# Depthwise convolution taps without diagonal products: ScalarE's products summed by accumulating transfers

## The chip, the core and the metric

The kernel runs on one core of one Trainium2 chip. Its engines are TensorE (PE; matmuls into PSUM), VectorE (DVE), ScalarE (ACT), GpSimd (POOL) and SyncE (SP, which issues transfers); each takes its instructions in the order of its own queue and waits where an operand is not there. The metric is the device time of one execution in microseconds, lower is better.

## What is computed

A trunk of two layers over a sequence of 1024 frames with 1024 channels, all in float32. Layer 0 mixes with a Conformer convolution module, layer 1 with chunkwise retention; each is followed by a squared-ReLU MLP of width 4096, and each sub-layer is normed and modulated by a conditioning vector. What the change touches is in layer 0:

```
u = h @ w_pw1 + b_pw1                     # 1024 -> 2048
a, g = split(u);  u = a * sigmoid(g)      # gate
u = depthwise causal convolution of u over 31 frames, per channel, + b_dw
u = silu(layernorm(u) * ln_g + ln_b)
y = u @ w_pw2 + b_pw2
x = x + g1 * y;  h = modulate(rmsnorm(x));  x = x + g2 * (relu(h @ w1)**2 @ w2)
```

## The kernel before

Channels lie on the 128 partitions, in 8 tiles; frames lie along a row, in two halves of 512. A float32 matmul is made of three: every weight block of 128 x 1024 is loaded by SP into `raw` (2 buffers), cast by ACT to a high part (L522), subtracted to a low part (L523), both into `whl` (9 buffers, two for a block), and `mm3` issues high x high, high x low and low x high (L258 to L260).

The first projection (pw1) makes, for a channel tile j and a half t, one unit `("u", j, t)`: 24 matmuls for the value, 24 for the gate, a sigmoid (L690) and the product (L699) that writes the unit's row, with 30 frames of the past ahead of it. The 31 taps of a unit are products of a shifted row with one weight per channel. Before, four engines share them:

- TensorE: the first `NPE[t][j]` taps as a matmul with a diagonal matrix, which ACT writes from the identity (`dg`, L718, L721), into a PSUM tile `acc`.
- VectorE: the middle taps, multiplied and added in one instruction (L730 begins a chain, L733 goes on), in two chains with a PSUM tile each.
- ACT and POOL: the last `NPOOL[t][j]` taps; ACT multiplies (`cacc` for the first, `prod` for the others, L738) and POOL adds each `prod` to `cacc` (L741).
- VectorE joins: `cacc` plus the first chain (L743), then plus the second, into the unit's own row (L744).

The 8 units of half 0 then go through the layer norm (mean, L753; scaling, L758), the second projection (pw2; its product is added to x in L782) and the MLP, of which 7 of 8 blocks run for half 0 alone (`mlp`: L804 to L809 make the hidden tiles, L818 adds to x) while the taps of half 1 are made. Modulation vectors are dot products of a 128 x 1024 block of `ada` with the condition: on VectorE in one instruction (L555), or on POOL (L552) with the sum on ACT (L553).

The order of all this is not written out: `Plan` takes every operation with an engine, a planned duration, a priority from the table `PR` and the buffers it needs (`RINGS`), plays them against each other, and issues them in the order that comes out. `NPOOL` and `NPE` share out the taps; `WPOOL` says that every n-th weight subtraction of a kind goes to POOL (0: none; `w1` there are the six pw1 blocks that are loaded a second time for half 1, so every 8th of them is none either); `M0POOL`, `M1POOL` and `MODPOOL` do the same for the dot products.

Of the kernel before, what the change touches and what calls it, by code (L numbers as in the profile page):

```python
# [58 lines left out]
PR = dict(h0=dict(A=504, V=930), x1=dict(D=1069, step=4), n1=dict(P=576, A=282, V=324), w0=dict(A=612, V=412, D=687, step=32), pw1=dict(P=778, step=0), glu=dict(A=841, V=327, G=591, step=32), taps0=dict(A=786, V=468, G=153, step=4), pw1h1=dict(P=1185, step=2), w1=dict(A=304, V=255, G=86, D=205, step=32), glu1=dict(A=252, V=67, step=0), halo=dict(A=354, step=2), dg=dict(P=989, step=16), mod2=dict(A=274, V=38, G=538, D=444, step=32), ln0=dict(P=555, A=52, V=38, step=2), y0=dict(D=218), pw2=dict(P=636, A=636, V=345, step=1), pw2w=dict(A=84, V=172, G=902, D=390, step=2), mod3=dict(A=488, V=349, G=92, D=558), nm0=dict(P=548, A=629, V=480, step=1), mod5=dict(A=322, V=96, G=271, D=571, step=4), mlp=dict(P=1064, A=793, V=339, G=552, D=587, step=0), taps1=dict(A=688, V=517, G=953), ln1=dict(P=690, A=1116, V=450, step=0), y1=dict(D=441), pw21=dict(P=615, A=508, V=193, step=2), pw2w1=dict(A=746, V=962, G=879, D=616, step=1), nm1=dict(P=328, A=268, V=867, step=0), m0=dict(A=641, V=571, G=43, D=769, step=1), m1=dict(A=486, V=187, G=818, D=0, step=1), wf=dict(A=976, V=291, D=847, step=32), G=dict(V=869, step=4))  # L59
WPOOL = dict(w0=0, w1=8, pw2=0, mlp=0, pw21=0)  # L60
M0POOL = (1, 2, 3)
M1POOL = (0, 4, 7)
# [4 lines left out]
class Plan:
# [139 lines left out]
class Trunk:  # L207
# [263 lines left out]
    def layer_conv(self):  # L471
# [236 lines left out]
        def taps(j, t, p):

            npool, npe = NPOOL[t][j], NPE[t][j]  # L710
            u = ("u", j, t)
# [4 lines left out]
            for s in range(npe):
                dg = k("dg", s)
                inorder("dg", "A", 0.293, p, lambda s=s, dg=dg: nc.scalar.activation(E[dg], self.ident, AF.Identity, scale=wv(s)),  # L718
                        r=["const"], w=[dg], a={dg: ("dg", dict(cols=P))})
# [1 line left out]
                inorder("acc" if s == 0 else ("pe", t, j), "P", 0.907, ("dg", 0), lambda s=s, dg=dg: nc.tensor.matmul(  # L721
                    E[k("acc", 0)], E[dg], sl(s), start=s == 0, stop=s == npe - 1), r=[dg, u], w=[k("acc", 0)], **first)
            begun = [npe > 0, False]
            for i, s in enumerate(range(npe, nd)):
                c = i % 2
                a = k("acc", c)
                if not begun[c]:
                    begun[c] = True
                    bias = self.v("b_dw", j) if c else 0.0
                    inorder("acc", "V", 0.68, p, lambda s=s, a=a, bias=bias: nc.vector.tensor_scalar(E[a], sl(s), wv(s), bias, ALU.mult, ALU.add),  # L730
                            r=[u, "const"], w=[a], a={a: ("acc", {})})
                else:
                    op("V", 0.68, p, lambda s=s, a=a: nc.vector.scalar_tensor_tensor(E[a], sl(s), wv(s), E[a], ALU.mult, ALU.add), r=[u], w=[a])  # L733
            ca = k("cacc")
            for i, s in enumerate(range(nd, TAPS)):
                pr = ca if i == 0 else k("prod", s)
                kind = "cacc" if i == 0 else "prod"
                inorder(kind, "A", 0.613, p, lambda s=s, pr=pr: nc.scalar.activation(E[pr], sl(s), AF.Identity, scale=wv(s)),  # L738
                        r=[u, "const"], w=[pr], a={pr: (kind, {})})
                if i:  # L740
                    op("G", 1.28, p, lambda pr=pr: nc.gpsimd.tensor_tensor(E[ca], E[ca], E[pr], ALU.add), r=[pr], w=[ca])  # L741
# [1 line left out]
            op("V", 0.62, p, lambda: nc.vector.tensor_tensor(E[ca], E[ca], E[a0], ALU.add), r=[a0], w=[ca])  # L743
            op("V", 0.62, p, lambda: nc.vector.tensor_tensor(E[u][:, :HALF], E[ca], E[a1], ALU.add), r=[ca, a1], w=[u])  # L744
# [569 lines left out]
```

## Time and profile before

| what | value |
|---|---|
| median of 3 runs | 2701.77 us (2699.62 to 2702.38) |
| the profiled execution | 2705.48 us, span 2703.6 us, mean granted TensorE clock 0.985 |
| busy of the span, PE / DVE / ACT / POOL | 2613.8 / 1635.2 / 1068.3 / 314.5 us |
| read from HBM, written | 251.46 MB, 6.29 MB |

Matmuls are pipelined, so a matmul's bar is longer than the time that it takes in a full stream, and a busy TensorE is not a full one. Shares over the whole span mix stages: the convolution layer ends before about 740 us, and what follows it is the same code before and after. A line number is that of the kernel which ran: the changed kernel's lines are 1 lower up to the taps and 3 lower behind them.

### The profile page before, as it was taken

The numbers are of one execution on the slowest core, as the hardware profiler recorded it, in microseconds if no ns is written. First come the engines' busy times: TensorE is split into PE (matmuls) and PEld (weight loads), VectorE is DVE, ScalarE is ACT, GpSimd is POOL, SyncE is SP. The second block draws the span as 40 slices with busy tenths as digits, with TensorE's granted clock in tenths as the row PEclk, the third lists the DMA queues.
The fourth block names the chain that finished last, engine by engine and source line by source line (L and its number), as shares of the span: only waits on it lengthen the run. The fifth ranks groups of instructions, "written<-read, shape, count | busy, mean of one in ns | idle before, by whom it ended". The sixth has DMA issues, their size and how long they took to land.

```text
span 2703.6 us, 29259 instructions
## 1 busy us (share of the span) xinstructions
PE 2613.8 (97%) x11450; PEld 2119.2 (78%) x11450; DVE 1635.2 (60%) x2237; ACT 1068.3 (40%) x1582; POOL 314.5 (12%) x212
## 2 busy tenths in 40 slices
PE   2989999999999999999999999999999999999997
PEld 1756777888787888788888888888888888888886
DVE  7799999965577445645545655365565333333336
ACT  4656866463222323343433633433543211222124
POOL 3677439100000000000000000000000000000002
PEclk6999999999999999999999999999999999999999
DMA  7522322242376223322222232232222111111112
GB/s 253 203 71 86 109 93 87 93 128 98 119 233 217 96 94 96 115 86 94 71 94 94 71 103 85 71 101 86 78 70 71 48 54 47 47 47 47 48 54 86
DMA packets 77197, 259.66 MB, mean 96 GB/s; under 512 B 8577, under 2 KB 11009, under 8 KB 76930
## 3 DMA queue, kind: packets, MB, share of 16 engines
q1 hardware_dynamic: 74240, 252.98, 28.6%
q10 hardware_dynamic: 2818, 4.81, 0.5%
q8 instruction: 90, 1.47, 0.2%
q14 instruction: 49, 0.40, 0.0%
HBM read 251.46 MB, written 6.29 MB: 95 GB/s over the span
## 4 chain that ended last, share of the span: by engine, by line
PE 84%; DVE 7%; DMA 4%; ACT 2%; issue 2%; POOL 1%; DVEq 0%; ACTq 0%; SPq 0%; POOLq 0%
PE mm L260 25%; PE mm L259 25%; PE mm L258 25%; DMA araw<-ada 3%; PE mm L964 2%; PE mm L963 2%; PE mm L962 2%; DVE acc L733 1%; POOL cacc L741 1%; DVE whl L523 1%; DVE araw L319 1%; PE ax L606 1%; PE acc L721 1%; DVE araw L555 0%; DVE hid L555 0%
## 5 line engine op out<-in xcount | busy, mean ns | idle before, releaser
L245 ACT CAST whl<-raw 128x1024 fp32r<-128x1024 f32 x264 | 277.0, 1050 | 809.7 <-PE mm L259 472.3
L246 DVE TENSOR_TENSOR whl<-raw,whl 128x1024 fp32r<-128x1024 f32 x264 | 322.7, 1223 | 403.5 <-ACT whl L245 302.7
L258 PE MATMUL mm<-hA,whl 128*128 128x512 f32 x1200 | 483.2, 403 | 44.5 <-ACT whl L522 41.7
L260 PE MATMUL mm<-hA,whl 128*128 128x512 f32 x1200 | 475.5, 396 | 8.5 <-DVE whl L523 6.3
L259 PE MATMUL mm<-hA,whl 128*128 128x512 f32 x1200 | 476.1, 397 | 1.9 <-DVE hA L542 1.7
L258 PE MATMUL mm<-hid,whl 128*128 128x512 f32 (+1 forms) x1024 | 394.3, 386 | 4.6 <-ACT hid L281 3.0
L259 PE MATMUL mm<-hid,whl 128*128 128x512 f32 (+1 forms) x1024 | 392.8, 384 | 1.1 <-DVE hid L282 1.0
L260 PE MATMUL mm<-hid,whl 128*128 128x512 f32 (+1 forms) x1024 | 392.8, 384 | 0.0
L258 PEld LDWEIGHTS mm<-hA,whl 128*128 128x128 f32 x1200 | 227.7, 190 | 101.3 <-ACT whl L522 43.5
L258 PE MATMUL mm<-hB,whl 128*128 128x512 f32 x704 | 279.3, 397 | 0.0
L260 PEld LDWEIGHTS mm<-hA,whl 128*128 128x128 f32 x1200 | 227.5, 190 | 63.8 <-DVE whl L523 9.8
L259 PE MATMUL mm<-hB,whl 128*128 128x512 f32 x704 | 274.4, 390 | 0.0
L260 PE MATMUL mm<-hB,whl 128*128 128x512 f32 x704 | 274.2, 390 | 0.0
L259 PEld LDWEIGHTS mm<-hA,whl 128*128 128x128 f32 x1200 | 227.6, 190 | 58.7 <-issue 5.3
L454 DVE SCALAR_TENSOR_TENSOR x<-mm,modb,x 128x512 f32<-128x512 f32 x192 | 143.8, 749 | 211.6 <-PE mm L260 211.0
L741 POOL TENSOR_TENSOR cacc<-cacc,prod 128x512 f32<-128x512 f32 x166 | 253.4, 1529 | 112.9 <-ACT prod L738 57.9
L1143 POOL TENSOR_SCALAR hA<-x,vec 128x256 f32<-128x256 f32 (+1 forms) x12 | 7.5, 622 | 2164.3 <-DVE x L454 2143.8
L258 PEld LDWEIGHTS mm<-hid,whl 128*128 128x128 f32 x1024 | 192.9, 189 | 45.6 <-ACT hid L281 5.9
L259 PEld LDWEIGHTS mm<-hid,whl 128*128 128x128 f32 x1024 | 192.9, 188 | 41.3 <-DVE hid L282 2.9
L260 PEld LDWEIGHTS mm<-hid,whl 128*128 128x128 f32 x1024 | 193.1, 189 | 37.1
L733 DVE SCALAR_TENSOR_TENSOR acc<-x,vec,acc 128x512 f32<-128x512 f32 x239 | 166.8, 746 | 2.8 <-PE acc L721 1.9
L259 PEld LDWEIGHTS mm<-hB,whl 128*128 128x128 f32 x704 | 132.2, 188 | 31.3 <-issue 2.9
(233 smaller groups left out, 3776.3 us busy)
## 6 DMA issues: line engine op xcount, KB each, us to landing
raw<-w SPq DMA_DIRECT2D x192, 512.0 KB, 3.5
araw<-ada SPq DMA_DIRECT2D x80, 512.0 KB, 4.3
raw<-pw SPq DMA_DIRECT2D x38, 512.0 KB, 4.1
raw<-rqk SPq DMA_DIRECT2D x32, 512.0 KB, 3.5
raw<-rv SPq DMA_DIRECT2D x32, 512.0 KB, 3.5
raw<-rgate SPq DMA_DIRECT2D x32, 512.0 KB, 3.5
raw<-rout SPq DMA_DIRECT2D x32, 512.0 KB, 3.5
x<-x SPq DMA_DIRECT2D x32, 256.0 KB, 3.2
```

The costliest lines, as they stand in the source:

```text
L245: nc.scalar.copy(hi[i], raw[:, i * W : i * W + W])
L246: nc.vector.tensor_tensor(lo[i], raw[:, i * W : i * W + W], hi[i].bitcast(F32), ALU.subtract)
L258: nc.tensor.matmul(out, whi, rhi, start=start, stop=False)
L259: nc.tensor.matmul(out, whi, rlo, start=False, stop=False)
L260: self.last_mm = nc.tensor.matmul(out, wlo, rhi, start=False, stop=stop)
L319: i = nc.vector.scalar_tensor_tensor(raw, raw, 1.0, self.cond, ALU.mult, ALU.mult, accum_out=out)
L454: nc.vector.scalar_tensor_tensor(x, ps, g2[:, n : n + 1], x, ALU.mult, ALU.add)
L733: op("V", 0.68, p, lambda s=s, a=a: nc.vector.scalar_tensor_tensor(E[a], sl(s), wv(s), E[a], ALU.mult, ALU.add), r=[u], w=[a])
L741: op("G", 1.28, p, lambda pr=pr: nc.gpsimd.tensor_tensor(E[ca], E[ca], E[pr], ALU.add), r=[pr], w=[ca])
L962: nc.tensor.matmul(vps[jt], hh[0], wh, start=kt == 0, stop=False)
L963: nc.tensor.matmul(vps[jt], hh[0], wl, start=False, stop=False)
L964: nc.tensor.matmul(vps[jt], hh[1], wh, start=False, stop=kt == KT - 1)
```

## The change

- No diagonal products: `NPE`, `dg` and their code are gone.
- ACT's products begin two sums (`cacc`, taps 30 and 29; the convolution's bias comes in with the first), and each further product is added to one of them, in turn, by a transfer that POOL issues and that accumulates in SBUF (L723 in the new kernel). A sum's transfers follow one another: each waits until the one before has landed. `cacc` has 5 buffers instead of 2.
- VectorE's two chains begin on these sums: the first tap of each reads `cacc` from SBUF and writes `acc` in PSUM (L734), the others go on in PSUM (L731), the last writes the unit's row (L729), and one addition (L741) instead of two joins the chains.
- The shares: ACT's and POOL's taps go from 91 + 91 (half 0 and 1) to 71 + 77, TensorE's from 43 + 10 to none, VectorE's from 114 + 147 to 177 + 171. Transfers are 56 + 61.
- Other shares: POOL takes 35 weight subtractions, where it had none (every 2nd of the MLP's and of half 0's pw2, every 3rd of `w1`'s, every 8th of half 1's pw2), 3 instead of 6 of the first 16 dot products and 16 instead of 10 of the others.
- The plan's table of priorities and the time from which half 1 of x may be loaded are new, the plan counts 4.8 us from the end of POOL's issue to the landing, and POOL's issue doesn't take the SBUF port in the plan. So the order changes on every engine.

POOL's queue, where the first taps' sums stand. In the kernel before, one addition follows another onto one sum, `cacc_465` (names are tiles with their number):

```order
L552 TENSOR_TENSOR araw_382<-araw_382,cond_81 128x1024
L741 TENSOR_TENSOR cacc_465<-cacc_465,prod_472 128x512
L741 TENSOR_TENSOR cacc_465<-cacc_465,prod_480 128x512
L741 TENSOR_TENSOR cacc_465<-cacc_465,prod_494 128x512
L741 TENSOR_TENSOR cacc_465<-cacc_465,prod_499 128x512
```

In the changed kernel, the transfers onto the two sums of unit 2 (519 and 524) alternate, with dot products between:

```order
L723 DMA cacc_519<-prod_532 128x512
L723 DMA cacc_524<-prod_537 128x512
L723 DMA cacc_519<-prod_546 128x512
L723 DMA cacc_524<-prod_554 128x512
L551 TENSOR_TENSOR araw_563<-araw_563,cond_81 128x1024
L551 TENSOR_TENSOR araw_575<-araw_575,cond_81 128x1024
L723 DMA cacc_519<-prod_594 128x512
L723 DMA cacc_524<-prod_611 128x512
```

What POOL worked on in place, it now only issues, and two sums of a unit are under way at once.

VectorE's queue at the end of half 0's taps (unit `x_124_396` before, `x_109_337` after, each the eighth). Before, the unit's chains begin on their own and the sum comes in last, in L743:

```order
L730 TENSOR_SCALAR acc_1790<-x_124_396,vec_63 128x512
L602 TENSOR_TENSOR sum_1111<-sum_1111,x_123_394 128x512
L733 SCALAR_TENSOR_TENSOR acc_1790<-x_124_396,vec_63,acc_1790 128x512 x4
L730 TENSOR_SCALAR acc_1825<-x_221_824,vec_63 128x512
L733 SCALAR_TENSOR_TENSOR acc_1825<-x_221_824,vec_63,acc_1825 128x512 x3
L733 SCALAR_TENSOR_TENSOR acc_1778<-x_124_396,vec_63,acc_1778 128x512 x5
L733 SCALAR_TENSOR_TENSOR acc_1825<-x_221_824,vec_63,acc_1825 128x512 x3
L743 TENSOR_TENSOR cacc_1776<-cacc_1776,acc_1778 128x512
L744 TENSOR_TENSOR x_124_396<-cacc_1776,acc_1790 128x512
```

After, the seventh unit's last tap and its one addition, and then the eighth's chains, which open with the sums:

```order
L731 SCALAR_TENSOR_TENSOR acc_1661<-x_108_334,vec_63,acc_1661 128x512
L729 SCALAR_TENSOR_TENSOR x_108_334<-x_108_334,vec_63,acc_1668 128x512
L741 TENSOR_TENSOR x_108_334<-x_108_334,acc_1661 128x512
L734 SCALAR_TENSOR_TENSOR acc_1792<-x_109_337,vec_63,cacc_1559 128x512
L734 SCALAR_TENSOR_TENSOR acc_1799<-x_109_337,vec_63,cacc_1565 128x512
L731 SCALAR_TENSOR_TENSOR acc_1792<-x_109_337,vec_63,acc_1792 128x512
```

The sums have moved from the end of a unit's taps to their start, and with them VectorE's wait for them: 23 taps of the eighth unit stand behind it, where there were 10 that didn't need it.

The diff, with the tables of priorities left out:

```
-X1_AT = 70
-RINGS = dict(raw=2, tmp=4, araw=2, whl=9, hid0=4, sum=2, prod=4, cacc=2, dg=6)
+X1_AT = 90
+RINGS = dict(raw=2, tmp=4, araw=2, whl=9, hid0=4, sum=2, prod=4, cacc=5)
 FILL = 2
-PW21_AT = 4
-NPOOL = ((15, 13, 14, 3, 15, 9, 11, 11), (14, 13, 13, 12, 2, 11, 14, 12))
-NPE = ((6, 8, 6, 6, 1, 0, 6, 10), (6, 0, 0, 0, 0, 1, 3, 0))
+PW21_AT = 6
+NPOOL = ((1, 10, 10, 11, 11, 7, 13, 8), (14, 19, 3, 7, 3, 10, 4, 17))
...
-WPOOL = dict(w0=0, w1=8, pw2=0, mlp=0, pw21=0)
-M0POOL = (1, 2, 3)
-M1POOL = (0, 4, 7)
-MODPOOL = dict(m2=2, m3=0, m4=2, m5=3)
+WPOOL = dict(w0=0, w1=3, pw2=2, mlp=2, pw21=8)
+M0POOL = (1, 6)
+M1POOL = (7,)
+MODPOOL = dict(m2=1, m3=0, m4=0, m5=1)
...
-                    t = max([free[e], o[7], port if o[8] else 0.0] + [end[d] + self.lat(ops[d][0], e) for d in o[4]])
+                    t = max([free[e], o[7], port if o[8] else 0.0] + [end[d] + ops[d][9] + self.lat(ops[d][0], e) for d in o[4]])
...
 
         def taps(j, t, p):
 
-            npool, npe = NPOOL[t][j], NPE[t][j]
+            npool = NPOOL[t][j]
             u = ("u", j, t)
             sl = lambda s: E[u][:, s : s + HALF]
             wv = lambda s: self.v("w_dw", j * TAPS + s)
             k = lambda *a: ("t", j, t) + a
+            for i in range(npool):
+                s, c = TAPS - 1 - i, i % 2
+                ca = k("cacc", c)
+                pr = ca if i < 2 else k("prod", s)
+                kind = "cacc" if i < 2 else "prod"
+                bias = self.v("b_dw", j) if i == 0 else 0.0
+                inorder(kind, "A", 0.613, p, lambda s=s, pr=pr, bias=bias: nc.scalar.activation(E[pr], sl(s), AF.Identity, scale=wv(s), bias=bias),
+                        r=[u, "const"], w=[pr], a={pr: (kind, {})})
+                if i > 1:
+                    op("G", 0.95, p, lambda pr=pr, ca=ca: nc.gpsimd.dma_start(E[ca], E[pr], accum_op=ALU.add), r=[pr], w=[ca], late=4.8)
             nd = TAPS - npool
-            for s in range(npe):
-                dg = k("dg", s)
-                inorder("dg", "A", 0.293, p, lambda s=s, dg=dg: nc.scalar.activation(E[dg], self.ident, AF.Identity, scale=wv(s)),
-                        r=["const"], w=[dg], a={dg: ("dg", dict(cols=P))})
-                first = dict(a={k("acc", 0): ("acc", {})}) if s == 0 else {}
-                inorder("acc" if s == 0 else ("pe", t, j), "P", 0.907, ("dg", 0), lambda s=s, dg=dg: nc.tensor.matmul(
-                    E[k("acc", 0)], E[dg], sl(s), start=s == 0, stop=s == npe - 1), r=[dg, u], w=[k("acc", 0)], **first)
-            begun = [npe > 0, False]
-            for i, s in enumerate(range(npe, nd)):
-                c = i % 2
+            for i in range(nd):
+                s, c = nd - 1 - i, i % 2
                 a = k("acc", c)
-                if not begun[c]:
-                    begun[c] = True
-                    bias = self.v("b_dw", j) if c else 0.0
+                if s == 0:
+                    op("V", 0.68, p, lambda a=a: nc.vector.scalar_tensor_tensor(E[u][:, :HALF], sl(0), wv(0), E[a], ALU.mult, ALU.add), r=[a], w=[u])
+                elif i > 1:
+                    op("V", 0.68, p, lambda s=s, a=a: nc.vector.scalar_tensor_tensor(E[a], sl(s), wv(s), E[a], ALU.mult, ALU.add), r=[u], w=[a])
+                elif c < npool:
+                    ca = k("cacc", c)
+                    inorder("acc", "V", 0.68, p, lambda s=s, a=a, ca=ca: nc.vector.scalar_tensor_tensor(
+                        E[a], sl(s), wv(s), E[ca], ALU.mult, ALU.add), r=[u, "const", ca], w=[a], a={a: ("acc", {})}, lock=True)
+                else:
+                    bias = self.v("b_dw", j) if c == npool == 0 else 0.0
                     inorder("acc", "V", 0.68, p, lambda s=s, a=a, bias=bias: nc.vector.tensor_scalar(E[a], sl(s), wv(s), bias, ALU.mult, ALU.add),
                             r=[u, "const"], w=[a], a={a: ("acc", {})})
-                else:
-                    op("V", 0.68, p, lambda s=s, a=a: nc.vector.scalar_tensor_tensor(E[a], sl(s), wv(s), E[a], ALU.mult, ALU.add), r=[u], w=[a])
-            ca = k("cacc")
-            for i, s in enumerate(range(nd, TAPS)):
-                pr = ca if i == 0 else k("prod", s)
-                kind = "cacc" if i == 0 else "prod"
-                inorder(kind, "A", 0.613, p, lambda s=s, pr=pr: nc.scalar.activation(E[pr], sl(s), AF.Identity, scale=wv(s)),
-                        r=[u, "const"], w=[pr], a={pr: (kind, {})})
-                if i:
-                    op("G", 1.28, p, lambda pr=pr: nc.gpsimd.tensor_tensor(E[ca], E[ca], E[pr], ALU.add), r=[pr], w=[ca])
-            a0, a1 = k("acc", 0), k("acc", 1)
-            op("V", 0.62, p, lambda: nc.vector.tensor_tensor(E[ca], E[ca], E[a0], ALU.add), r=[a0], w=[ca])
-            op("V", 0.62, p, lambda: nc.vector.tensor_tensor(E[u][:, :HALF], E[ca], E[a1], ALU.add), r=[ca, a1], w=[u])
+            a = k("acc", nd % 2)
+            op("V", 0.62, p, lambda: nc.vector.tensor_tensor(E[u][:, :HALF], E[u][:, :HALF], E[a], ALU.add), r=[a], w=[u])
```

More of the change, by code (lines that the diff above doesn't have):

```diff
@@ L58 @@
 BEGIN = dict(P=3.0, A=2.5, V=2.0, G=1.0, D=1.8)
-PR = dict(h0=dict(A=504, V=930), x1=dict(D=1069, step=4), n1=dict(P=576, A=282, V=324), w0=dict(A=612, V=412, D=687, step=32), pw1=dict(P=778, step=0), glu=dict(A=841, V=327, G=591, step=32), taps0=dict(A=786, V=468, G=153, step=4), pw1h1=dict(P=1185, step=2), w1=dict(A=304, V=255, G=86, D=205, step=32), glu1=dict(A=252, V=67, step=0), halo=dict(A=354, step=2), dg=dict(P=989, step=16), mod2=dict(A=274, V=38, G=538, D=444, step=32), ln0=dict(P=555, A=52, V=38, step=2), y0=dict(D=218), pw2=dict(P=636, A=636, V=345, step=1), pw2w=dict(A=84, V=172, G=902, D=390, step=2), mod3=dict(A=488, V=349, G=92, D=558), nm0=dict(P=548, A=629, V=480, step=1), mod5=dict(A=322, V=96, G=271, D=571, step=4), mlp=dict(P=1064, A=793, V=339, G=552, D=587, step=0), taps1=dict(A=688, V=517, G=953), ln1=dict(P=690, A=1116, V=450, step=0), y1=dict(D=441), pw21=dict(P=615, A=508, V=193, step=2), pw2w1=dict(A=746, V=962, G=879, D=616, step=1), nm1=dict(P=328, A=268, V=867, step=0), m0=dict(A=641, V=571, G=43, D=769, step=1), m1=dict(A=486, V=187, G=818, D=0, step=1), wf=dict(A=976, V=291, D=847, step=32), G=dict(V=869, step=4))
@@ L60 @@
-WPOOL = dict(w0=0, w1=8, pw2=0, mlp=0, pw21=0)
-M0POOL = (1, 2, 3)
-M1POOL = (0, 4, 7)
-MODPOOL = dict(m2=2, m3=0, m4=2, m5=3)
+PR = dict(h0=dict(A=393, V=433), x1=dict(D=305, step=4), n1=dict(P=917, A=524, V=640), w0=dict(A=1043, V=452, D=349, step=0), pw1=dict(P=288, step=8), glu=dict(A=25, V=114, G=873, step=16), taps0=dict(A=152, V=678, G=682, step=0), pw1h1=dict(P=775, step=0), w1=dict(A=778, V=695, G=1108, D=442, step=32), glu1=dict(A=0, V=0, step=2), halo=dict(A=11, step=16), dg=dict(P=685, step=1), mod2=dict(A=817, V=163, G=975, D=980, step=16), ln0=dict(P=61, A=236, V=847, step=1), y0=dict(D=217), pw2=dict(P=604, A=810, V=253, step=16), pw2w=dict(A=639, V=379, G=161, D=522, step=4), mod3=dict(A=336, V=302, G=353, D=821), nm0=dict(P=412, A=653, V=767, step=32), mod5=dict(A=705, V=597, G=819, D=978, step=4), mlp=dict(P=672, A=404, V=0, G=752, D=1034, step=0), taps1=dict(A=332, V=996, G=588), ln1=dict(P=105, A=257, V=947, step=0), y1=dict(D=393), pw21=dict(P=711, A=276, V=599, step=4), pw2w1=dict(A=257, V=971, G=801, D=576, step=8), nm1=dict(P=405, A=817, V=283, step=1), m0=dict(A=446, V=216, G=103, D=473, step=32), m1=dict(A=6, V=212, G=1164, D=355, step=32), wf=dict(A=251, V=397, D=1064, step=16), G=dict(V=583, step=0))
@@ L76, in __init__, with op @@
         self.all_users = {}
-    def op(self, eng, dur, prio, fn, r=(), w=(), a=None, after=(), hold=(), table=None, at=0.0, lock=False):
+    def op(self, eng, dur, prio, fn, r=(), w=(), a=None, after=(), hold=(), table=None, at=0.0, lock=False, late=0.0):
         i = len(self.ops)
@@ L96, in op @@
             self.all_users.setdefault(k, []).append(i)
-        self.ops.append((eng, dur, self.priority(prio, eng), fn, sorted(deps), a or {}, table, at, lock or eng == "G"))
+        self.ops.append((eng, dur, self.priority(prio, eng), fn, sorted(deps), a or {}, table, at, lock or (eng == "G" and not late), late))
         return i
@@ L186, in order @@
                 if not left[k] and k in home:
-                    freed[home[k]] = max(end[j] for j in self.all_users[k])
+                    freed[home[k]] = max(end[j] + ops[j][9] for j in self.all_users[k])
             for j in outs[i]:
@@ L475, in layer_conv @@
         cp = self.cstack.enter_context(tc.tile_pool(name="conv", bufs=1, reuse_waits="tile"))
-        self.tags.update({t: (cp, RINGS[t]) for t in ("sum", "prod", "cacc", "dg")})
+        self.tags.update({t: (cp, RINGS[t]) for t in ("sum", "prod", "cacc")})
         self.cond = self.t2("cond", cols=D)
```

## The prediction

> **What bounds the kernel now.** I read the parts of the page first, then busy time by stage, then groups by shape, then single instructions in order of time. The profiled execution took 2705.5 us, its span is 2703.6, and the median of the runs is 2701.8, 3.7 less; I sum against the profiled one and take the saving off the median.
>
> Busy time by stage (PE, weight loads, DVE, ACT, POOL, granted clock, DMA share, GB/s):
>
> ```profile
> 0.00:70.00 70.00, 21.34 (x33) 9.42 (x34) 54.78 (x73) 29.36 (x47) 26.15 (x21) 0.62 0.70 244
> 70.00:135.00 65.00, 61.22 (x239) 45.67 (x238) 46.89 (x52) 42.91 (x69) 42.45 (x22) 0.96 0.62 211
> 135.00:305.00 170.00, 155.17 (x576) 108.81 (x574) 164.42 (x224) 108.07 (x182) 118.42 (x81) 0.98 0.22 75
> 305.00:541.00 236.00, 235.58 (x997) 187.19 (x998) 230.59 (x317) 146.86 (x211) 110.67 (x71) 1.00 0.31 101
> 541.00:740.00 199.00, 197.19 (x851) 160.26 (x850) 117.72 (x151) 80.65 (x108) 0.00 (x0) 0.99 0.35 113
> 740.00:2703.60 1963.60, 1943.34 (x8762) 1607.86 (x8760) 1020.79 (x1424) 660.44 (x969) 16.81 (x18) 1.00 0.27 87
> ```
>
> Only the first 740 us hold anything that the change touches. From 135 to 305 VectorE works 164.4 of 170 us: it has the taps of half 0, and nothing after them can start until they are done. TensorE looks nearly full there too, but single instructions say otherwise:
>
> ```profile
> 402.60 0.39 PE L258 MATMUL mm<-hid,whl 128*128 128x512 f32 x1
> 402.82 0.39 PE L259 MATMUL mm<-hid,whl 128*128 128x512 f32 x1
> 134.54 5.31 PE L721 MATMUL acc<-x,dg 128*128 128x512 f32 x12
> 303.83 0.39 PE L260 MATMUL mm<-hB,whl 128*128 128x512 f32 x1
> 305.19 0.49 PE L258 MATMUL mm<-hA,whl 128*128 128x512 f32 x1 [0.98 <-ACT hA L536]
> ```
>
> A matmul's bar is 0.39 us, but in a full stream the next begins 0.23 us later; a diagonal product's instruction takes 5.31/12 = about 0.43. The 848 instructions up to 305 hold 86 diagonal ones (43 products, two each), so TensorE needed some 762 x 0.227 + 86 x 0.43 = 210 us and lost about 95, half of them before its first matmul. At 305 the second projection (pw2 of half 0) starts, as the layer norm's last scalings arrive:
>
> ```profile
> 301.28 3.38 DVE L758 SCALAR_TENSOR_TENSOR x<-x,vec,ax 128x512 f32<-128x512 f32 x5
> 308.34 0.74 DVE L758 SCALAR_TENSOR_TENSOR x<-x,vec,ax 128x512 f32<-128x512 f32 x1
> ```
>
> After 305 TensorE is busy 235.6 of 236 and then 197.2 of 199: from there it is the bound. So two clocks count: when pw2 can start (VectorE's), and how much TensorE has left then.
>
> **The change, part by part.** Groups of the first 760 us, with mean ns of one:
>
> ```profile
> L741 POOL TENSOR_TENSOR cacc<-cacc,prod 128x512 f32<-128x512 f32 x166 | 253.4, 1529 | 112.9 <-ACT prod L738 57.9 <-ACT cacc L738 43.7
> L733 DVE SCALAR_TENSOR_TENSOR acc<-x,vec,acc 128x512 f32<-128x512 f32 x239 | 166.8, 746 | 2.8 <-PE acc L721 1.9
> L523 DVE TENSOR_TENSOR whl<-raw,whl 128x1024 fp32r<-128x1024 f32 x92 | 123.6, 1350 | 37.3 <-PE mm L259 10.9 <-ACT whl L522 10.9 <-issue 9.7
> L738 ACT ACTIVATE prod<-x,vec 128x512 f32<-128x512 f32 x166 | 115.4, 717 | 19.6 <-POOL cacc L741 19.2
> L721 PE MATMUL acc<-x,dg 128*128 128x512 f32 x106 | 47.3, 593 | 3.8 <-DVE modb L565 2.5 <-DVE x L744 1.4
> L555 DVE SCALAR_TENSOR_TENSOR araw<-araw,cond 128x1024 f32<-128x1024 f32 x22 | 34.9, 1593 | 8.0 <-DMA araw<-ada 8.0
> L552 POOL TENSOR_TENSOR araw<-araw,cond 128x1024 f32<-128x1024 f32 x10 | 28.1, 2808 | 43.0 <-DMA araw<-ada 35.0 <-DVE acc L733 8.1
> L718 ACT ACTIVATE dg<-ident,vec 128x128 f32<-128x128 f32 x53 | 19.2, 391 | 7.6 <-PE acc L721 7.5
> L555 DVE SCALAR_TENSOR_TENSOR hid<-hid,cond 128x1024 f32<-128x1024 f32 x10 | 18.5, 1862 | 0.4 <-DMA hid<-ada 0.4
> L743 DVE TENSOR_TENSOR cacc<-cacc,acc 128x512 f32<-128x512 f32 x16 | 10.9, 680 | 0.3
> ```
>
> 1. TensorE loses the 53 products: 106 x 0.43 = 45.6 us. But 86 of the instructions (37 us) lie before 305, where TensorE waits for VectorE; removing them there only makes it wait longer. What counts for certain is the 20 after it: 8.6 us.
>
> 2. VectorE gets taps: 348 instead of 261 in all. Counted in its order up to the eighth scaling of half 0 (L758): 187 taps instead of 131, 8 closing additions instead of 16, 19 wide weight subtractions instead of 20, 29 modulation dots instead of 32, 3 others more. A run of these costs 3.38/5 = 0.67 us each, a closing addition about 0.6, a wide one 1.15: 37.5 - 4.8 - 1.2 - 3.4 + 2 = 30 us more. Taken alone this starts pw2 30 us later.
>
> 3. ACT loses 53 diagonals and 34 products of the 182 (166 + 16), 19 + 24 us. It is not the bound in any stage above, so I cost that at nothing; VectorE covers it.
>
> 4. POOL stops adding: 253 us of two-operand work go, 117 transfers to issue come. Both engines stretch when both read two SBUF operands:
>
> ```profile
> 84.60 21.86 POOL L741 TENSOR_TENSOR cacc<-cacc,prod 128x512 f32<-128x512 f32 x10 [7.79 <-ACT prod L738]
> 87.40 2.31 DVE L523 TENSOR_TENSOR whl<-raw,whl 128x1024 fp32r<-128x1024 f32 x1
> 94.08 2.30 DVE L555 SCALAR_TENSOR_TENSOR araw<-araw,cond 128x1024 f32<-128x1024 f32 x1
> L523 DVE TENSOR_TENSOR whl<-raw,whl 128x1024 fp32r<-128x1024 f32 x20 | 24.4, 1222 | 26.5 <-PE mm L259 10.9 <-issue 9.7 <-PE mm L260 4.8
> L319 DVE SCALAR_TENSOR_TENSOR araw<-araw,cond 128x1024 f32<-128x1024 f32 x5 | 6.0, 1221 | 4.0 <-DMA araw<-ada 3.9
> L658 DVE SCALAR_TENSOR_TENSOR G<-mod,adb,vec 128x1 f32<-128x1 f32 x8 | 7.2, 945 | 0.0
> 24.99 0.59 DVE L658 SCALAR_TENSOR_TENSOR G<-mod,adb,vec 128x1 f32<-128x1 f32 x4
> ```
>
> The fourth and fifth rows are 600 to 740, where POOL is idle: 1222 and 1221 ns. So VectorE lost 92 x 0.128 + 22 x 0.372 + 10 x 0.641 = 26 us on wide rows, and 6 on the eight L658 (four cost 0.59 together when undisturbed). Ahead of pw2 POOL had 187 us of work (26.2 + 42.5 + 118.4); the new order leaves it 19 modulation products and one or two weight subtractions there, some 21 x 2.8 = 59 us, a third. I take back two thirds of 32: 22 us.
>
> 5. VectorE's idle time before 135 is 15.2 + 18.1 us. In the new order 37 taps (25 us) stand ahead of the fifth gate product, where there were none, and only 3 instead of 6 of the first 16 dots are POOL's. I take 15 us back, and 7 from an earlier first matmul. Bounds: 0, and 33 for both.
>
> 6. The wait that is added: the first tap of each of VectorE's two chains reads a sum that transfers have to finish, and stands in VectorE's queue ahead of all that follows, scalings, weight subtractions and gate products included. Of half 0, the longer of two lanes over units 2 to 8 is 4 + 4 + 5 + 5 + 3 + 6 + 3 = 30 transfers, each waiting for the landing of the one before. Two pairs of units overlap in POOL's order; I count 27 steps. VectorE's own work between the second gate product and the eighth unit's first tap is 145 us by the same prices, with stretching and gaps 155 to 165. So a step of up to about 5.9 us is covered; beyond that each 0.1 us costs 2.7. No accumulating transfer is in this trace. The nearest are:
>
> ```profile
> std<-tmp SPq DMA_DIRECT2D x8, 256.0 KB, 2.0
> x<-x SPq DMA_DIRECT2D x32, 256.0 KB, 3.2
> hid<-ada SPq DMA_DIRECT2D x16, 512.0 KB, 5.0
> ```
>
> Low end 2.0 (these 256 KB, one way); high end 5.0 (512 KB, what source and destination make together, in a busy stage) plus 1.5 for the issue, if it holds POOL as long as the addition that it replaces: 6.5. I take 5.7, near the high end, since it too moves 512 KB in. The Trainium skill ("DMA: Bandwidth & Descriptors", Anatomy of one DMA) fits 2.0 us + bytes/436e3 for a transfer issued by GpSimd, 2.6 for 256 KB; by it the chains would be well hidden, and the sum the same. ACT's products wait for a free one of 4 buffers behind the same landings, with weight casts queued behind them; that is the same step length.
>
> 7. VectorE hands 35 weight subtractions to POOL, most in the MLP. Up to the sixteenth L809 VectorE's work is then 438 us against 433 before, so the 30 us of part 2 are given back there. On POOL each takes about 2.8 us (L552's row) behind transfers that wait. Nine buffers of halves cover that; a block is due every 24 x 0.227 = 5.4 us.
>
> **Sum.** pw2's start: + 30 - 22 - 22 = 14 us earlier, so about 291. After it TensorE has 8.6 us less to do and stays the bound. 2705.5 - 14 - 8.6 = 2682.9; off the median, 2679.
>
> **Rivals.** (a) The transfers' chains bind: for it, a step near 6 uses all the cover. At 6.7 the 22 us are gone, at 7.5 it is 27 x 1.6 - 22 = 21 us slower, 2723. It decides from 6.7 on. Against it, both nearest rows of 256 KB are at 3.2 or under. 0.23. Part of it is a rule that would lengthen the step: a stretch like that of L741 (2.15 instead of 1.28 us beside L523) on every issue adds 0.9 to each of 27 steps, 24 us, and ends at 2703. The Trainium skill ("SBUF — State Buffer", Who interferes with whom) says that descriptors for GpSimd's transfers can't be written while VectorE is in a two-port mode. By that page the two-input forms that fill this stage take only the read side, so I give it 0.06 of the 0.23. (b) POOL's subtractions come late and TensorE waits in the MLP: 35 x 1 us at worst, 2710; 0.07. (c) No change: pw2 starts 8 us later, since part 4's relief is small, and the 8.6 are used up; 2702, 0.13. (d) More: the start-up is freed of POOL altogether and pw2 starts 30 us or more earlier; 33 + 32 - 30 = 35, plus 8.6: 2658; 0.15. The floor is all 45.6 us and 10 of start-up, 2646.
>
> **How the numbers follow.** The forecast has 0.42. Faster is forecast and (d), 0.57; same is (c), 0.13; slower is (a) and (b), 0.30 (0.2%, 5.4 us, is about what a measurement can tell from no change). The range leaves out a tenth on each side: 2650 at the bottom, 2724 at the top, a step of 7.5. The forecast alone is 2664 to 2694.
>
> **What would show it.** In the profile after: L721 and L718 gone; L731 the largest group on VectorE; its first taps' (L734) wait for transfers under 10 us in all; the first pw2 matmul (first hA row after the last hB block) near 291; the span from there to the end 8 to 9 us shorter than 2703.6 - 305.2. Wrong if L734 waits tens of us for cacc's transfers, if a step is over 6.7, or if weight subtractions on POOL release TensorE.

## The result and the profile after

The changed kernel takes 2714.67 us (median of 5 runs, 2710.01 to 2716.95), the kernel before 2700.90 beside it: ratio 1.0049, 95% interval 1.0035 to 1.0064. It is slower, by some 13 us; 2679 was forecast. Its profiled execution took 2716.05 us with a span of 2714.3, 10.7 more than before. Two executions that ran in a slower state are in no median of this document: one of d_h1_taps (2932.5 us) and one of the kernel before (5358.1 us).

Busy time by stage of the changed kernel, columns as in the prediction:

```profile
0.00:70.00 70.00, 29.12 (x84) 18.37 (x85) 58.30 (x100) 26.85 (x37) 8.75 (x15) 0.73 0.82 282
70.00:135.00 65.00, 50.03 (x186) 35.02 (x184) 50.92 (x77) 38.54 (x60) 31.51 (x24) 0.89 0.88 243
135.00:305.00 170.00, 129.41 (x498) 100.07 (x499) 159.34 (x218) 96.97 (x150) 75.54 (x66) 0.85 0.76 166
305.00:541.00 236.00, 229.88 (x977) 183.65 (x976) 212.05 (x298) 120.35 (x166) 88.84 (x66) 0.99 0.61 146
541.00:740.00 199.00, 188.47 (x808) 152.42 (x807) 111.02 (x143) 84.35 (x114) 29.15 (x12) 0.97 0.31 97
740.00:2714.30 1974.30, 1950.56 (x8797) 1613.66 (x8796) 1027.98 (x1436) 662.64 (x972) 16.81 (x18) 1.00 0.28 88
```

From 135 to 305 TensorE has 26 us less of busy time, most of it the diagonal products that are gone, and VectorE is still at 159 of 170. What is new stands in the next two rows: TensorE, which had been busy 235.6 of 236 and 197.2 of 199 us, now misses 6 and 10.5. The transfers show in the DMA share, 0.76 for 0.22.

The new groups up to 760 us, busy and mean ns, then idle time before them and its releasers:

```profile
L723 POOL DMA_DIRECT2D cacc<-prod x117 | 103.2, 983 | 184.2 <-DMA cacc<-prod 73.5 <-ACT prod L720 64.6 <-ACT cacc L720 14.7
L522 POOL TENSOR_TENSOR whl<-raw,whl 128x1024 fp32r<-128x1024 f32 x35 | 87.2, 2491 | 250.4 <-PE mm L259 81.9 <-PE mm L258 72.2 <-ACT whl L521 53.4
L720 ACT ACTIVATE prod<-x,vec 128x512 f32<-128x512 f32 x117 | 81.3, 717 | 34.3 <-DMA cacc<-prod 34.3
L734 DVE SCALAR_TENSOR_TENSOR acc<-x,vec,cacc 128x512 f32<-128x512 f32 x31 | 26.2, 877 | 2.7 <-POOL araw L551 1.4 <-DMA cacc<-prod 1.2
```

The last row is the wait that I had feared most: 31 first taps wait 2.7 us in all, 1.2 of it for a landing. POOL (73.5) and ScalarE (34.3) are what waits for landings.

To see where the 10 us are I count TensorE's lost time: time since the start less 0.429 us for each diagonal instruction and 0.2275 for every other matmul. At 305 us it is 95.7 before and 130.7 after. 36.9 us of diagonal work (86 x 0.429) had gone by then, so TensorE is only 1.9 us further on. From 305 to 744 it loses 29.8 us for 10.9: 18.9 more. The 20 later products save 8.6, the rest of the kernel loses 1.6 more. -1.9 - 8.6 + 18.9 + 1.6 = +10.0, and the last matmul ends at 2704.3 for 2694.3. The first pw2 matmul stands at 300.77, 4.4 us earlier, where I had 14.

More than half of the 18.9 is one wait. What TensorE waited for from 305 to 744 us in the changed kernel (us, times, longest):

```profile
PE mm L257 <- ACT hid L804: 11.5, 3, 10.5
PE mm L259 <- POOL whl L522: 1.9, 1, 1.9
```

And ScalarE in order of time before that wait ends:

```profile
568.25 0.59 ACT L804 CAST hid<-mm 128x512 fp32r<-128x512 f32 x1 [1.69 <-DVE mm L802]
568.73 1.05 ACT L521 CAST whl<-raw 128x1024 fp32r<-128x1024 f32 x1
569.79 1.28 ACT L760 ACT_TABLE_LOAD   x1
571.09 0.72 ACT L760 ACTIVATE tmp<-x,vec 128x512 f32<-128x512 f32 x1
571.85 0.62 ACT L535 CAST hB<-tmp 128x512 fp32r<-128x512 f32 x1
...
580.04 0.72 ACT L760 ACTIVATE tmp<-x,vec 128x512 f32<-128x512 f32 x1
580.79 0.62 ACT L535 CAST hB<-tmp 128x512 fp32r<-128x512 f32 x1
581.31 5.00 ACT L777 ACTIVATE x<-x,gb 128x512 f32<-128x512 f32 x8
586.22 0.57 ACT L801 ACTIVATE tmp<-mm 128x512 f32<-128x512 f32 x1
587.56 0.58 ACT L804 CAST hid<-mm 128x512 fp32r<-128x512 f32 x1 [0.77 <-DVE mm L802]
```

ScalarE never idles from 568.7 to 586.2, and none of that is what TensorE then waits for: eight silus and casts of half 1's layer norm and eight residual biases stand in its queue ahead of the relu (L801) of the MLP's fourth hidden tile. TensorE had finished that tile's products at 571.5, ran out of other work at 577.7 and goes on at 588.2.

### The profile page after: what moved, and what is told of

The parts are those of the page before. It is cut to its first block, busy times and chain, and to the rows that moved or that the text cites. A ratio compares the mean times of both kernels' runs of the same rounds, so it can differ in the third digit from the quotient of the medians.

```text
span 2714.3 us, 29029 instructions
## 1 busy us (share of the span) xinstructions
PE 2577.5 (95%) x11344; PEld 2103.2 (77%) x11344; DVE 1619.6 (60%) x2267; ACT 1029.7 (38%) x1497; POOL 250.6 (9%) x201
## 4 chain that ended last, share of the span: by engine, by line
PE 79%; DVE 6%; DMA 4%; ACT 2%; issue 1%; POOL 0%; DVEq 0%; ACTq 0%; POOLq 0%; SPq 0%
PE mm L258 24%; PE mm L259 24%; PE mm L257 24%; DMA araw<-ada 3%; PE mm L961 2%; PE mm L959 2%; PE mm L960 2%; DVE acc L731 1%; DVE araw L318 1%; DMA raw<-w 1%; DVE whl L522 1%; DVE hB L541 1%; DVE whl L245 0%; ACT whl L521 0%; POOL whl L522 0%
## 5 line engine op out<-in xcount | busy, mean ns | idle before, releaser
L257 PE MATMUL mm<-hA,whl 128*128 128x512 f32 x1200 | 479.0, 399 | 42.7 <-ACT whl L521 36.4
L257 PE MATMUL mm<-hid,whl 128*128 128x512 f32 (+1 forms) x1024 | 394.8, 386 | 19.2 <-ACT hid L804 11.5
L731 DVE SCALAR_TENSOR_TENSOR acc<-x,vec,acc 128x512 f32<-128x512 f32 x300 | 205.2, 747 | 0.0
L257 PEld LDWEIGHTS mm<-hB,whl 128*128 128x128 f32 x704 | 133.6, 190 | 42.1 <-ACT hB L539 12.3
L259 PEld LDWEIGHTS mm<-hB,whl 128*128 128x128 f32 x704 | 133.6, 190 | 39.7 <-DVE whl L522 11.9
```

The costliest lines, as they stand in the source:

```text
L257: nc.tensor.matmul(out, whi, rhi, start=start, stop=False)
L259: self.last_mm = nc.tensor.matmul(out, wlo, rhi, start=False, stop=stop)
```

## Experiments

"Lost" is TensorE's lost time from 305 to 744 us by the count above; pw2 is the start of its first matmul. Each ratio is to the kernel before, run beside it (its medians in these were 2702.6 to 2703.4).

| kernel | us | ratio, 95% interval | pw2 | lost |
|---|---|---|---|---|
| before | 2700.9 | | 305.2 | 10.9 |
| changed | 2714.7 | 1.0049 (1.0035 to 1.0064) | 300.8 | 29.8 |
| a_prod_wide | 2716.1 | 1.0046 (1.0034 to 1.0058) | 301.1 | 31.1 |
| b_h0_taps | 2708.5 | 1.0022 (1.0013 to 1.0032) | 293.1 | 29.9 |
| c_before_diag0 | 2704.1 | 1.0002 (0.9994 to 1.0011) | 302.9 | 12.0 |
| d_h1_taps | 2714.0 | 1.0038 (1.0024 to 1.0053) | 301.0 | 32.0 |
| e_ln1 | 2701.9 | 0.9997 (0.9988 to 1.0006) | 300.2 | 20.2 |
| f_short | 2696.6 | 0.9980 (0.9971 to 0.9989) | 285.2 | 27.5 |
| g_no_pool_mods | 2702.3 | 1.0000 (0.9991 to 1.0009) | 287.7 | 30.0 |
| i_oldtab | 2743.1 | 1.0148 (1.0134 to 1.0162) | 313.7 | 50.7 |
| k_self | 2710.4 | 1.0027 (1.0015 to 1.0038) | 293.9 | 32.4 |
| p_half_mods | 2700.2 | 0.9993 (0.9984 to 1.0001) | 300.0 | 20.0 |
| n_sub_dve | 2710.7 | 1.0031 (1.0020 to 1.0043) | 302.0 | 26.6 |
| q_x70 | 2694.2 | 0.9974 (0.9963 to 0.9984) | 288.9 | 18.1 |
| h_x70 | 2704.9 | 1.0009 (1.0001 to 1.0018) | 292.4 | 31.0 |
| u_before_x90 | 2746.7 | 1.0161 (1.0147 to 1.0174) | 306.0 | 37.5 |
| v_x50 | 2713.7 | 1.0046 (1.0032 to 1.0059) | 314.2 | 30.4 |

Where VectorE's time goes up to 305 us I split in three: idle before an instruction, its undisturbed duration (the lower quartile of its form where the next follows at once), and the rest, stretch. Before: 38.5, 215.3 and 50.8 us. Changed: 36.4, 247.7 and 21.1.

**a_prod_wide**: is ScalarE held by its four product buffers?

```
+            if tag == "prod" and kw.pop("t") == 0:
+                self.alt = not getattr(self, "alt", False)
+                if self.alt:
+                    return self.t2("hid0", cols=2 * HALF)[:, :HALF]
```

> The changed kernel (2714.7 us) with the products of half 0 spread over eight buffers instead of four (every second one goes to the ring of the MLP's hidden tiles, which half 0 does not use); the order on every engine stays. Theory 1: ScalarE is held at a product until the transfer of the fourth one before has landed (27 us of such waits before 305 us), gate sigmoids and weight casts behind it come late, and this is what kept VectorE idle for the 36 us that did not go away; then those waits shrink below 8 us, pw2 starts 6 to 10 us earlier (291 to 295 us instead of 300.8), and the time is about 2707. Theory 2: ScalarE had slack there and VectorE's own work is what reaches to pw2; then the waits shrink as well, pw2 moves by under 3 us, and the time stays within 2712 to 2716.

ScalarE's 27 us of waits for landings are gone, and nothing else moved: 2716.1, pw2 at 301.1. ScalarE then waits elsewhere (for POOL's dot products 19.2 us instead of 10.8, for loads of pw1 22.6 instead of 17.1). Theory 1 falls.

**b_h0_taps**: does VectorE's work reach to pw2?

```
-  elif i > 1: op("V", ... scalar_tensor_tensor(E[a], sl(s), ...))
+  elif i > 1: op("V", ... None if t == 0 and 2 <= i < 6 else scalar_tensor_tensor(...))
```

> The changed kernel with four of VectorE's chained taps left out in each of the eight units of half 0: 32 taps, 32 x 0.68 = 22 us of VectorE's work ahead of pw2; nothing else moves. Theory 2 (VectorE's work reaches to pw2): pw2 starts 15 to 22 us earlier, 279 to 286 us, and the time falls by 14 to 22 us to 2693 to 2700. Theory 1 (VectorE waits for a held ScalarE, which this leaves as it is): most of the 22 us turns into more idle time of VectorE, pw2 starts under 8 us earlier, time 2707 to 2714. Rival 3: what follows pw2 (weight loads, ScalarE's casts) does not come earlier, so that an earlier pw2 is given back in new waits of TensorE by 740 us; then pw2 moves as in theory 2 but the time falls by less than half of it.

Of 22 us, 7.7 reach pw2, and the ratio falls by 0.0027, some 7 us; VectorE's idle time up to 305 rises from 36.4 to 51.7. These are the numbers of theory 1, but its cause, the four buffers, had fallen in a_prod_wide; theory 2, the full 22 us, falls here. So a third of the work that was left out is on the path, and the rest is paced by something else that feeds VectorE. Rival 3 falls: what pw2 gained arrived.

**c_before_diag0**: what were TensorE's products worth ahead of pw2?

```
-  lambda: nc.tensor.matmul(E[acc], E[dg], sl(s), ...)
+  lambda: None if t == 0 and s else nc.tensor.matmul(...)
```

> The kernel before (2700.9 us) with 36 of the 43 diagonal products of half 0 left out (one per unit stays; their ScalarE diagonals stay): 36 x 0.86 = 31 us of TensorE's work ahead of pw2, nothing else moves. My working said that TensorE has slack there and its products are worth nothing: time 2698 to 2701.5, pw2 starts within 3 us of 305. Rival: TensorE's work delays the gates and the units' ends; then pw2 starts 10 to 25 us earlier and the time falls by as much, to 2676 to 2691, which would mean that the change lost what it took from TensorE somewhere else.

Nothing: 31 us of matmuls taken out, ratio 1.0002. TensorE's lost time at 305 rises by 29.3.

**d_h1_taps**: is it half 1's added work on VectorE?

```
-  elif i > 1: op("V", ... scalar_tensor_tensor(E[a], sl(s), ...))
+  elif i > 1: op("V", ... None if t == 1 and 2 <= i < 5 else scalar_tensor_tensor(...))
```

> The changed kernel with three of VectorE's chained taps left out in each of the eight units of half 1: 24 taps, 24 x 0.68 = 16 us less of VectorE's work between 305 and 640 us (about what half 1 gained against the kernel before: 171 taps for 147). Theory 4: that added work is why TensorE waits 28 us for late results between 305 and 744 us where it waited 9 before; then these waits fall by 8 to 16 us and the time is 2699 to 2707. Theory 5: the waits come from ScalarE, whose weight casts stand in front of its relu and wait for loads whose raw buffers POOL's subtractions hold (casts waited 64 us for loads in all, 40 before); then the waits of TensorE stay above 22 us and the time is 2711 to 2715.

The ratio moved by 0.0011, inside both intervals, and the 588 us wait stayed as it was (10.7 us, at 590): theory 4 falls. The numbers are those of theory 5, but its cause is not borne out below (n_sub_dve).

**e_ln1**: two numbers in the table of priorities.

```
-ln1=dict(P=105, A=257, ...)  pw21=dict(P=711, A=276, ...)
+ln1=dict(P=105, A=450, ...)  pw21=dict(P=711, A=450, ...)
```

> The changed kernel with two numbers of the table of priorities changed (ScalarE's in ln1 257 to 450, in pw21 276 to 450, so both stand behind the MLP's 404): the eight silus, eight casts and eight residual biases of half 1's layernorm, 16 us on ScalarE at 570 to 586 us, no longer stand in one block ahead of the relu of the fourth hidden tile. Theory 6 (the order of the new tables put a wait where there was none): TensorE's 10.5 us wait at 588 us (for the hidden tile's cast) goes to under 2 us, and the time is 2703 to 2708. Theory 4 or 5 (half 1 has more work than VectorE or ScalarE can do beside the MLP): the wait moves to a later hidden tile or to half 1's own pw2, and the time stays within 2711 to 2716.

2701.9, 0.0052 of the ratio or 14 us better, and level with the kernel before. TensorE from 575 to 608 us, in the changed kernel:

```profile
575.00:608.00 33.00, 22.47 (x90) 17.81 (x89) 14.37 (x20) 17.36 (x26) 4.30 (x2) 0.84 0.39 127
```

and in e_ln1:

```profile
575.00:608.00 33.00, 33.00 (x145) 27.01 (x144) 18.67 (x25) 21.09 (x30) 7.28 (x3) 1.00 0.49 160
```

The wait is gone, and with it a dip of the granted clock (0.84) that followed it. Theory 6 is shown, with a time a little under its range: the relu now comes after the first silu, at 571.9. The other runs agree: a wait of 10.5 to 10.7 us for this cast stands in every one that has the changed kernel's table as it is (a, b, d, f, g, h, k), and in none that has these two numbers changed (e, n, p, q, v).

**f_short** and **k_self**: the transfers' bytes, and the chain that they form.

```
-  nc.gpsimd.dma_start(E[ca], E[pr], accum_op=ALU.add)
+  nc.gpsimd.dma_start(E[ca][:, :64], E[pr][:, :64], accum_op=ALU.add)   # f_short
+  nc.gpsimd.dma_start(E[pr], E[pr], accum_op=ALU.add)                   # k_self
```

> The changed kernel with every accumulating transfer cut from 512 columns to 64 (most of the products' sum is left out): 117 transfers with an eighth of their bytes, same number of issues, same order. Theory 7: the transfers' own time and traffic (landing 5.0 us, DMA share 0.76 from 135 to 305 us against 0.22 before, weight landings 4.4 us) hold ScalarE's products, the first taps and the loads, and so pw2: then landings fall to 2 to 3.5 us, the loads' to about 3.6, pw2 starts 5 to 10 us earlier, and the time is 2702 to 2709. Theory 2 (VectorE's own work): pw2 moves by under 2 us, time 2711 to 2716.

> The changed kernel with each of the 117 transfers adding the product onto the product itself instead of onto the unit's sum (the sums miss these products): same 256 KB, same number, same places on POOL, but no transfer waits any more for the landing of the one two before it in its sum's chain (POOL waited 47.6 us in 20 places for that from 50 to 300 us, with its products of the modulation rows and its weight subtractions queued behind), and no first tap waits for a sum. Cutting the transfers to 64 columns gave 18 us. Theory 9 (the chain of additions into two sums, holding POOL's queue): most of that comes back here too, pw2 starts 10 to 16 us before 300.8 and the time is 2696 to 2704. Theory 10 (the traffic itself: 16 DMA engines shared with the loads): loads and landings stay as slow, pw2 moves by under 4 us, time 2709 to 2716.

Transfers of the changed kernel, of f_short and of k_self (count, KB each, median us to landing):

```profile
cacc<-prod POOLq DMA_DIRECT2D x117, 256.0 KB, 5.0
```

```profile
cacc<-prod POOLq DMA_DIRECT2D x117, 32.0 KB, 3.1
```

```profile
prod<-prod POOLq DMA_DIRECT2D x117, 256.0 KB, 6.0
```

POOL's waits from 50 to 300 us, in the changed kernel and in f_short:

```profile
POOL cacc L723 <- DMA cacc<-prod: 47.6, 20, 6.4
```

```profile
POOL cacc L723 <- DMA cacc<-prod: 15.4, 7, 4.8
```

f_short gained more than expected, 18 us, with pw2 15.6 earlier; VectorE's idle time up to 305 falls from 36.4 to 23.9. So the transfers do hold half 0, in part through POOL: a transfer that waits for the landing of the one two before it stands in front of POOL's dot products and weight subtractions. k_self has no such wait and full bytes: pw2 6.9 earlier, the ratio 0.0022 (6 us) down. That lies between theories 9 and 10 for pw2, and in theory 10's range for the time. By pw2's start, the chain is worth about 7 us; the other 9 are a difference, put down to the bytes and to what they do to other transfers. How those reach VectorE is not shown; the traces say that its wait for gate sigmoids (L689, 50 to 300 us) is 2.7 us in f_short, 8.4 in k_self and 11.1 in the changed kernel.

**g_no_pool_mods**

```
-  lambda: nc.gpsimd.tensor_tensor(E[raw], E[raw], self.cond, ALU.mult)
+  lambda: None if kind in (2, 5) else nc.gpsimd.tensor_tensor(...)
```

> The changed kernel with POOL's 16 products of the modulation rows 2 and 5 left out (16 x 2.43 = 39 us of two-operand work of POOL before 305 us, most of it at 93 to 190 us; ScalarE's sums over those rows stay). Theory 8: these hold VectorE's port (a subtraction of 0.7 us took 4.16 us at 146 us while one of them ran) and the transfers queue behind them on POOL; then VectorE's stretch before 305 us falls from 21 to under 10 us, ScalarE's waits for landings from 27 to under 15, pw2 starts 6 to 12 us earlier and the time is 2701 to 2708. Theory 2: VectorE's idle time grows by what the stretch loses, pw2 moves by under 3 us, time 2710 to 2716.

The time came out as theory 8 has it, with pw2 13.1 us earlier, one more than its range. VectorE's stretch up to 305 went from 21.1 to 11.8, not quite under 10; its idle time did not grow (35.7), against theory 2. ScalarE's waits for landings rose to 36 us instead of falling, so that part of theory 8 is wrong: 9 us of the gain are VectorE's stretch, and the rest, perhaps POOL's own time, is not separated.

**p_half_mods**: half of these to VectorE, on top of e_ln1.

```
+  vec = kind in (2, 5) and kt % 2
+  nc.vector.scalar_tensor_tensor(..., accum_out=col()) if vec else nc.gpsimd.tensor_tensor(...)
```

> The kernel with the mended order of half 1's layernorm (2701.9 us) and eight of POOL's 16 products of the modulation rows 2 and 5 done by VectorE with the sum in one instruction of 1.15 us, at the same places; the other eight stay. Leaving all 16 out gave 12.4 us in the changed kernel. Theory 8 (POOL's two-operand work beside VectorE, and the transfers queued behind it): about half of that, 6 us, comes, less what 8 x 1.15 = 9.2 us of VectorE's work costs at the third of its price that 22 us of left-out taps showed (3 us): 2697 to 2701, faster than before. Theory 2 (VectorE's work counts in full): 2703 to 2709.

2700.2 is in theory 8's range, but its interval overlaps e_ln1's, and pw2 did not move (300.0): undecided.

**n_sub_dve**: POOL's 35 weight subtractions, on top of e_ln1.

```
-  eng = nc.vector if low == "V" else nc.gpsimd
+  eng = nc.vector
```

> The kernel with the mended order of half 1's layernorm (2701.9 us) and POOL's 35 weight subtractions done by VectorE at the same places of the order (35 x 1.15 = 40 us more for VectorE, 35 x 2.4 = 84 us less for POOL). Theory 5 (these hold the raw buffers, ScalarE's casts and so the MLP): ScalarE's waits for weight loads fall from 64 to under 45 us, TensorE's remaining waits between 305 and 744 us (20 us by the count of its work) fall by 6 or more, time 2692 to 2698. Rival: the nine weight buffers cover POOL's slower subtractions, and VectorE's 40 us come on top where it has no slack: 2702 to 2712.

The rival's range, 9 us worse. ScalarE's casts wait 51.0 us for the MLP's loads, 47.7 in e_ln1: POOL does not hold the buffers. Theory 5 falls, and handing these to POOL was right.

**i_oldtab**: the new taps under the old tables.

```
-PR, WPOOL, M0POOL, M1POOL, MODPOOL, X1_AT = 90, PW21_AT = 6
+the same names with the values of the kernel before
```

> The new taps (same split of the taps, same accumulating transfers, no diagonal products) with the tables of before: the priorities, POOL's shares of the weight subtractions and modulation rows, and the two due times; the planner orders anew. It parts the mechanism from the tables that came with it. If the new taps themselves cost what was lost: 2710 or more, with over 20 us of TensorE's waits between 305 and 744 us. If the tables cost it (POOL's subtractions, the order of half 1's layernorm): 2685 to 2704, waits there under 14 us, pw2 at 295 to 305 us. Theory 5 in particular (raw buffers held by POOL's 35 subtractions): ScalarE's casts wait under 45 us for loads, 64 in the changed kernel.

It is 28 us slower than the changed kernel; TensorE waits 34.6 us at 293 us for a sum of half 0's layer norm, and 9.3 and 10.4 us at 562 and 574 for half 1's. That reads like the first case, yet the same taps reach 2694 below. The run only shows that tables and shares belong together. Against theory 5 it adds that ScalarE's casts wait 66.6 us for the MLP's loads here, where POOL has no subtraction of the MLP.

**q_x70, h_x70, u_before_x90, v_x50**: the time from which half 1's x may be loaded, with e_ln1's edit (q, v) and without (h), and in the kernel before (u).

```
-X1_AT = 90
+X1_AT = 70     # q_x70, h_x70; v_x50: 50; u_before_x90: 70 to 90
```

> The kernel with the mended order of half 1's layernorm (2701.9 us) and the second half's activations loaded from 70 us on, as in the kernel before, instead of 90. TensorE waits 9, 3, 11 and 6 us at 123 to 151 us for the norm of half 1. Theory 11 (half 1's norm is late and holds what follows): these waits shrink by 15 us or more, and pw2 starts 4 to 8 us earlier: 2694 to 2698. Theory 3 (TensorE's time before pw2 is slack): the waits move to other places ahead of pw2, pw2 moves by under 2 us, 2700 to 2704.

> The changed kernel with one number changed: the due time of the second half's activations 70 instead of 90; half 1's layernorm stays in its block ahead of the relu. If the two causes are independent: pw2 starts at 288 to 291 us as with both mended, the 10.5 us wait of TensorE stays (at about 577 us), and the time is 2703 to 2708. If the earlier start only leads into a longer wait at the relu: 2711 to 2716.

> The kernel before (2702 us) with the due time of the second half's activations 90 instead of 70, nothing else. If the late load costs by itself (half 1's norm and its units late, VectorE idle): 2708 to 2715, pw2 starts 6 to 12 us later than 305. If it costs only in the changed kernel, where the loads share the engines with 60 accumulating transfers before 305 us: within 2700 to 2705, pw2 within 3 us of 305.

> The changed kernel with half 1's layernorm mended and the second half's activations due at 50 us instead of 70 (2694.2 us) or 90 (2701.9 us). If half 1's norm is what holds the stage: the remaining waits of TensorE for it (6.0 us at 127, 7.3 us at 140) go and pw2 starts 3 to 8 us before 289: 2686 to 2691. If the eight loads then push the first weights and modulation rows back on the load queue: the first gates come 2 to 5 us later, pw2 moves by under 2 us or later, 2693 to 2702.

q_x70 beats both kernels: 2694.2, ratio 0.9974. Its stages, and its first pw2 matmul:

```profile
135.00:305.00 170.00, 138.20 (x547) 106.84 (x548) 166.09 (x233) 108.80 (x170) 78.67 (x67) 0.89 0.79 176
305.00:541.00 236.00, 228.72 (x976) 182.16 (x975) 211.56 (x296) 114.27 (x156) 89.60 (x67) 1.00 0.60 142
541.00:740.00 199.00, 197.82 (x860) 161.05 (x859) 112.61 (x148) 85.75 (x117) 26.65 (x11) 1.00 0.38 119
```

```profile
288.85 0.80 PE L257 MATMUL mm<-hA,whl 128*128 128x512 f32 x1 [6.30 <-ACT hA L535]
```

VectorE works 166 of 170 us from 135 to 305 (159 in the changed kernel), its idle time up to 305 is 23.3 instead of 36.4, and by the count TensorE stands 13.0 us further on at 305 than before. Theory 11 holds in the main: TensorE's waits for half 1's norm before pw2 fall from 31.1 us in e_ln1 to 16.8, and pw2 starts 11.3 us earlier, more than expected. h_x70 keeps the wait at the relu (10.6 us, at 580) and gains 11 us, so there are two causes; they overlap somewhat (11 and 14 alone, 20 together).

But the number is no price of its own. At 50 the same kernel is at 2713.7, with pw2 at 314, outside both expectations. In the kernel before, 90 costs 44 us, far outside both expectations, though pw2 starts at 306.0: TensorE has done 12 us less by 305 and loses 26 us more up to 406. Its largest new wait, from 60 to 420 us, is for a weight block (19.5 us of it at 226):

```profile
PE mm L260 <- DVE whl L523: 25.3, 4, 19.5
```

Each of these numbers re-sorts hundreds of instructions. That moved the time by 8 to 44 us, where the change moved it by 13.

## Why the prediction was wrong

Part 1 was right: ahead of pw2 the diagonal products were worth nothing (c_before_diag0). Part 2 was right in size, 32 us of added work for 30, but I charged it in full; b_h0_taps puts a third of what it left out of VectorE's work on the path. Part 4 was right in kind and low: stretch fell by 30 us, not 22. Part 7 held: nine buffers cover POOL's subtractions; TensorE waited for one once, for 1.9 us.

**Part 5 is the term that failed ahead of pw2.** I took back 22 us of VectorE's idle time, with a lower bound of nothing, from taps that stand earlier in its order. Idle time fell by 2.1, from 38.5 to 36.4. Counted up to each kernel's own pw2, work rose by 28.0, stretch fell by 29.8 and idle time by 2.8, so pw2 came 4.6 earlier, where I had 30 - 22 - 22. Work put earlier in a queue fills a gap only if its own inputs are there: VectorE's idle before 135 us fell from 33.3 to 23.5 and came back behind it, 5.2 to 12.9 from 135 to 305. Under q_x70's order, with the same taps, the term is 15.2; with the transfers cut short (f_short) it is 14.6.

**Part 6 priced the transfers in the wrong queue.** The step was close (landing 5.0 us, 5.7 taken) and the cover real: first taps waited 2.7 us, so rival (a) did not happen where I put it. I had named VectorE's queue, and ScalarE's in one sentence as "the same step length"; ScalarE's waits are indeed worth nothing (a_prod_wide). The stretch that (a) put at 0.9 us on each issue was about 0.13: an issue took 0.98 us on average and 0.85 in the median. On POOL I counted dot products and issues as work, never what stands behind an issue that waits for a landing. That, with the bytes, is worth 15.6 us of pw2's start (f_short).

**The sum failed in its last line, "stays the bound".** I let TensorE run on after pw2 as before and subtracted 8.6. It lost 18.9 us more, 12.1 of them at 575 to 608 (10.5 the wait, the rest with the clock's dip). Part 3 costed ScalarE at nothing because it bounds no stage. But an engine with slack can still stand in the way for 16 us if its order puts a block ahead of the one instruction that TensorE waits for. The order showed that block; I had looked at the queues around the taps only. No rival named it: (a) and (b) gave the side, not the cause. That 2714.7 lies between 2650 and 2724 is luck, since the upper end comes from (a); so is (b)'s nearness (its 35 us on 2679 are 2714, not the 2710 written).

With these two orders mended the forecast's steps come out: pw2 at 288.9 (291 forecast), TensorE 13.0 us ahead at 305 (14), less 8.6, plus 7.2 of waits that remain and 0.6 after: -13.8 in the profile. The agreement is partly luck: up to its pw2, q_x70's work rose by 26.0, its stretch fell by 26.6 and its idle time by 15.9. The runs show 0.9974, about 7 us; the profiled execution of the kernel before lies 3 us above its median and q_x70's 2 below. Of the 7.2 us, 5.7 stand from 340 to 375 us (6.6 lost for 0.9), where the MLP begins: TensorE waits four times, 4.1 us in all, for normed rows, a weight cast and a subtraction on POOL (1.9).

## What to carry to other kernels

When a change comes with a new order, follow the bound engine's producers through every queue, those of idle engines too: a wait is set by what stands ahead of the needed instruction, not by how busy its engine is. A transfer that must follow another's landing holds all that is queued behind its issue. And before a mechanism is judged, it should be tried under more than one order: here the same taps ran in 2694 to 2743 us.

## What the runs showed of the hardware

- An accumulating transfer within SBUF of 256 KB lands 5.0 us after its issue, one of 32 KB after 3.1 (medians of 117). An estimate from these two: 2.8 us fixed and 0.85 us for every 100 KB. So an eighth of the bytes saves only 38%. The Trainium skill ("DMA: Bandwidth & Descriptors", Anatomy of one DMA) fits 2.0 us + bytes/436e3 to a transfer issued by GpSimd, by which an estimate for 256 KB is 2.6 us. The accumulating ones take about twice that here, with the loads beside them, so the measured 5.0 us is the number to use.
- VectorE's L541 (128 x 512), 0.74 us on average in its groups on `hA`, took 4.16 us at 146.2 us, beside a two-operand product of POOL from 146.9 to 149.8.
